# A fourth early up tile and an instruction order written by hand between the first LayerNorm and the feed-forward block, in a one-core transformer layer

## The chip, the core and the metric

The kernel runs on one core of a Trainium2 chip. Its engines are TensorE (PE in the profile, with weight loads shown as PEld), VectorE (DVE), ScalarE (ACT), GpSimd (POOL) and SyncE (SP, which here only issues DMAs). The metric is the device time of one launch in microseconds (us), taken as the median of several runs. Lower is better.

## What is computed

One diffusion-transformer layer over 1024 tokens of width 1024: two attention branches, a gated merge, a residual with LayerNorm, and a convolutional SwiGLU feed-forward block with a second LayerNorm. The change lies between the first LayerNorm and the feed-forward block:

```python
x = _layer_norm(DEEPNORM_ALPHA * x + gate1 * y, ln1_g[l], ln1_b[l])
h = x * (1.0 + scale2) + shift2
y = _conv_ffn(h, w_up[l], conv_w[l], conv_b[l], w_down[l])
x = _layer_norm(DEEPNORM_ALPHA * x + gate2 * y, ln2_g[l], ln2_b[l])

def _conv_ffn(h, w_up, conv_w, conv_b, w_down):
    u = h @ w_up                       # 1024 x 5632
    ...                                # depthwise conv of width 3 over tokens, plus conv_b
    gate, val = jnp.split(u, 2, axis=-1)
    return (jax.nn.silu(gate) * val) @ w_down
```

All data is float32. Each matrix product is done as three matmuls (`mm3`, L89): both operands are split into a rounded high part and a low remainder, and high x high, high x low and low x high are added up. So every operand needs a cast on ScalarE (L82) and a subtraction on VectorE or GpSimd (L87 for weights, L1208 for activations) before TensorE can use it.

## The kernel before

**Layout.** Features lie on the 128 partitions and tokens along the free dimension. The hidden width 2816 of the feed-forward block is cut into 22 up tiles `j`; each has a gate part (`gv` = 0) and a value part (`gv` = 1), written `u0_j` and `u1_j` here. The first three (`NCL = 3`) are plain products, each part 8 x 2 x 3 matmuls of 512 tokens (`up_mm`, L1393). The other 19 are block tiles (`up_tile`, L1498): a 2 x 2 block scheme with seven products A11, S2, S1, S3, A12, S4, A22 of 12 matmuls each (`prod`, L1486) in place of eight. Their weight operands are sums of weight blocks (`wsums`, four additions on GpSimd), cast and split by `pairs` (L1477); their activation operands are the normalized activations `B` and sums of them, `T13` and `T24`, made by `build` (L1239).

**The stage of the change.** The output projection (`y_pair`) fills `z` in three token slices, 0:512, 512:768 and 768:1024 (`LN1_S`). For each slice `ln_steps` (L1144) takes sums by tiny matmuls, broadcasts mean and scale into a PSUM tile (L1174, tile `bca` in the pool tag `sml`, two banks), and then for each of eight feature tiles applies them on VectorE and GpSimd (L1182 to L1186), makes the high part and a copy `v` on ScalarE (L1202), and the low part (L1208). Meanwhile TensorE works on `u0_0`, `u1_0` and `u0_1` for the slices that are ready (L1431 to L1436). Their sums stand in the three two-bank PSUM slots of the tag `big`. After that come `u1_1`, `u0_2` and `u1_2` over all tokens (`up_conv`, L1406), each taking a `big` slot after the convolution (`conv3`, L1363) has read the earlier part there; `gated` (L1373) multiplies gate and value and stores them. The steps of `build` hang on a clock of matmul columns (`tick`, L1130, cost `BLD = 2400`). Then all of PSUM is given back and taken anew as eight single banks for the block tiles.

**Rings.** Raw weights go through three buffers `raw`; high and low weights through two rings of four (`w` and `wd`), which the plain parts and the block tiles share. A slot is filled again only after the matmuls that read it.

**What sets the order.** TensorE's order is written by hand from L1304 on. On the other engines and on the DMA queues a planner in the framework orders the instructions: it takes them by program order as their inputs become ready in its own simulation. On the chip each engine then runs its list strictly in order. `with tc.manual_schedule(engines=...)` turns the planner off for the named engines, so that these follow the program text.

Of the kernel before, what the change touches and what calls it, by code (L numbers as in the profile page):

```python
# [13 lines left out]
P = 128  # L14
D = 1024
T = 1024
# [53 lines left out]
def layer_kernel(  # L70
# [65 lines left out]
    def hput(*names):  # L136
        for n in names:
            hfree.append(hslot.pop(n))
# [865 lines left out]
    za = tc.alloc_tile_pool(name="za", bufs=1, side="right", reuse_waits="tile")  # L1004
    wq = tc.alloc_tile_pool(name="wq", bufs=1, side="right", reuse_waits="tile")
    ps3 = tc.alloc_tile_pool(name="ps3", bufs=1, space=PSUM, reuse_waits="tile")

    hfree += [(za, f"Z{n}") for n in range(16)]

# [4 lines left out]
        return ps3.tile([P, T], F32, tag="big", name=name, bufs=3)  # L1014

    def sml(name, w=512):
        return ps3.tile([P, w], F32, tag="sml", name=name, bufs=2)

    def weight(src, nm, n=8, tag="w", he=None, le=None, rtag="raw"):
        if rtag:  # L1020
# [268 lines left out]
    def up_weights(j, gv, which=None):  # L1289
        upw[j, gv] = wring(w_up[2 * j + gv], f"wu{gv}_{j}", le=nc.vector, which=which)  # L1290
# [72 lines left out]
    def conv3(t, u, c):  # L1363
        nc.scalar.activation(t, u, AF.Identity, bias=cvb[:, c:c + 1], scale=cvw[:, c, 1:2])
        nc.vector.scalar_tensor_tensor(out=t[:, 1:T], in0=u[:, 0:T - 1], scalar=cvw[:, c, 0:1], in1=t[:, 1:T],
                                       op0=ALU.mult, op1=ALU.add)
        nc.vector.scalar_tensor_tensor(out=t[:, 0:T - 1], in0=u[:, 1:T], scalar=cvw[:, c, 2:3],
                                       in1=t[:, 0:T - 1], op0=ALU.mult, op1=ALU.add)
# [37 lines left out]
    def up_conv(j):  # L1406
        cv = []
        for gv in (0, 1):
            up_mm(j, gv, [hsl(0), hsl(1)])
            if gv == 0:  # L1410
                hslot[f"c0_{j}"] = pool, tag = cs[j % 2]
                t = pool.tile([P, T], F32, tag=tag, name=f"c0_{j}", bufs=1)
            else:
                if j == NCL - 1:
                    hput("B3_1")
                    hfree.insert(0, hfree.pop())
# [5 lines left out]
        if j:  # L1422
            later.append(f"c1_{j}")
        else:
            hput(f"c1_{j}")

    up_weights(1, 0, 1)
    up_weights(1, 1, 1)
    for j, gv in ((0, 0), (0, 1), (1, 0)):
        up_start(j, gv)  # L1430
    for si, s in enumerate(LN1_S):  # L1431
        drain((len(LN1_S) - 1 - si) * (KT + 3))
        for j, gv in ((0, 0), (0, 1), (1, 0)):
            up_mm(j, gv, [s])
            if s.stop == T:
                ups[j, gv][2].add(HALF)  # L1436
    cs = [hfree.pop(0) for _ in range(2)]
    for k in range(4):
        pend += [(BLD, fn) for fn in build(k)]
    later = []  # L1440
    for j in range(NCL):
        up_conv(j)
    drain()
    hput(*[f"B{k}_1" for k in range(3)], *later)


    ps3.release()
    ps3 = tc.alloc_tile_pool(name="ps3u", bufs=1, space=PSUM, reuse_waits="tile")

    ubanks = list(PSU)  # L1450

    def bank(name):
        n = ubanks.pop(0)
        ubanks.append(n)
        return ps3.tile([P, HALF], F32, tag=f"u{n}", name=name)

    for n in range(8):
        ps3.tile([P, HALF], F32, tag=f"u{n}", name=f"u{n}")

    def wload(j):  # L1460
        wraw[j] = [post.tile([P, 8, P], F32, tag="raw", name=f"ru{gv}_{j}", bufs=3) for gv in (0, 1)]
        for gv in (0, 1):
            nc.sync.dma_start(wraw[j][gv], w_up[2 * j + gv])
# [12 lines left out]

    def pairs(j, *names):  # L1477
        for n in names:
            if (j, n) not in wsrc:
                continue  # L1480
            pool, tag = ((wq, "w"), (post, "wd"))[npair[0] % 2]
            npair[0] += 1
            t = wtile[j, n] = pool.tile([P, 2, HALF], R32, tag=tag, name=f"w{n}_{j}", bufs=4)
            split(wsrc.pop((j, n)), t[:, 0], t[:, 1], nc.scalar, getattr(nc, UE[list(prods).index(n)]))

    def prod(j, n, o, start, stop):  # L1486
        w = wtile.pop((j, n))
        for k in range(4):
            c = slice(k * P, (k + 1) * P)
            mm3(o, (w[:, 0, c], w[:, 1, c]), opnd(prods[n], k), start and k == 0, stop and k == 3, not start)  # L1490
            tick(HALF / 0.8)

    def add(o, p, q, e=nc.vector):
        e.tensor_tensor(out=o, in0=p, in1=q, op=ALU.add)
# [1 line left out]
    lohalf, hihalf = slice(0, HALF), slice(HALF, T)  # L1496

    def up_tile(j):  # L1498
        a, b, c, d = (bank(f"{n}{j}") for n in "abcd")
# [7 lines left out]
        prod(j, "S2", b, True, True)  # L1507
        add(ve, b, pe)
        prod(j, "S1", c, True, True)
        nc.scalar.copy(uv[:, hihalf], c)  # L1510
        pairs(j, "A12", "S4", "A22")
        if j + 1 < NF:
            wload(j + 1)
            wsums(j + 1, tm)
        prod(j, "S3", d, True, True)
        add(uv[:, hihalf], d, uv[:, hihalf])
        add(uv[:, hihalf], uv[:, hihalf], ve, nc.gpsimd)
        pairs(j + 1, "A11")
        prod(j, "A12", a, False, True)
        nc.scalar.copy(ug[:, lohalf], a)  # L1520
        prod(j, "S4", c, False, True)
        add(ug[:, hihalf], c, ve)
        conv3(tg, ug, j)
        nc.scalar.activation(tg, tg, AF.Silu)
# [7 lines left out]
    wload(NCL)  # L1532
    wsums(NCL, tm)
    pairs(NCL, "A11", "S2", "S1", "S3")
    for j in range(NCL, NF):
        if j == NF - 1:
            dnext()
        up_tile(j)
# [338 lines left out]
```

## Time and profile before

| what | value |
|---|---|
| time, median of 3 runs | 1578.76 us (1578.74 to 1580.79) |
| the profiled execution, its own time | 1578.46 us |
| its span, first to last instruction | 1576.7 us |
| VectorE busy 946 to 957 us | 11.0 of 11 us |
| VectorE busy 957 to 979 us | 18.8 of 22 us |

The profile is one execution. Its page gives sums over the whole span; the views of stretches, of the chain of waits and of the order of time are cut out of the same record. Matmuls overlap in the pipeline, so the distance from one start to the next says how fast TensorE goes, not the duration of one. An idle time is put down to the engine whose semaphore came last. The stage in question runs from about 903 us (first plain product) to 979 us (first block product).

### The profile page before, as it was taken

Reading aid. Unit: us, or ns where it says so; the run is one execution under the profiler, and the core shown is the slowest. Engines: PE = TensorE matmul, PEld = TensorE weight load, DVE = VectorE, ACT = ScalarE, POOL = GpSimd, SP = SyncE. Lnnn points to the kernel's source line nnn. Section 1 sums busy time; section 2 is a strip of 40 time slices with the busy share of each in tenths; the row PEclk is TensorE's granted clock in tenths of the full one; section 3 lists DMA queues with packets and bytes.
Section 4 is the critical chain, followed back from the end, with each engine's and each line's share of the span. In section 5 each row is a group of like instructions: output and inputs, shape, how many; then the busy total and the mean of one; then the engine's idle time right before and its main releaser. Section 6 shows DMA issues by size and latency. Waiting matters only on the chain.

```text
span 1576.7 us, 22297 instructions
## 1 busy us (share of the span) xinstructions
PE 1538.4 (98%) x7804; PEld 1283.1 (81%) x7804; DVE 1199.0 (76%) x1768; ACT 813.8 (52%) x1450; POOL 740.2 (47%) x728
## 2 busy tenths in 40 slices
PE   9999999999999999989999999999999999999997
PEld 7888888888877787777688988888888888888887
DVE  6677976548888677788674788788888887657884
ACT  5323123368887667688430564444444444435552
POOL 0355423526666556555342454566667774021121
PEclk9999999999999999999999999999999999999998
DMA  9776662322247555440550222323334446996821
GB/s 372 270 234 234 224 232 90 110 79 59 63 127 158 130 134 132 115 87 18 179 174 27 92 69 96 118 96 117 109 108 118 110 113 186 367 266 210 258 101 54
DMA packets 112528, 230.00 MB, mean 146 GB/s; under 512 B 12992, under 2 KB 27840, under 8 KB 112320
## 3 DMA queue, kind: packets, MB, share of 16 engines
q1 hardware_dynamic: 97184, 199.72, 38.1%
q0 software_dynamic: 10400, 20.19, 8.4%
q10 hardware_dynamic: 4832, 8.68, 1.5%
q8 instruction: 61, 1.00, 0.3%
q14 instruction: 51, 0.42, 0.1%
HBM read 177.35 MB, written 65.86 MB: 154 GB/s over the span
## 4 chain that ended last, share of the span: by engine, by line
PE 87%; DVE 5%; ACT 3%; issue 2%; POOL 1%; DMA 0%; SPq 0%; DVEq 0%; ACTq 0%; POOLq 0%
PE ptr L611 5%; PE p L90 4%; PE p L91 4%; PE p L92 4%; PE g L90 4%; PE g L92 4%; PE g L91 4%; PE b L92 3%; PE b L91 3%; PE b L90 3%; PE av L632 2%; PE s L494 2%; PE av L633 2%; PE d L92 2%; PE c L92 2%; PE a L92 2%
## 5 line engine op out<-in xcount | busy, mean ns | idle before, releaser
L621 DVE TENSOR_TENSOR ptl<-ptr,pth 128x512 fp32r<-128x512 f32 x188 | 124.5, 684 | 28.0 <-ACT pth L620 26.0
L611 PE MATMUL ptr<-ident,p 128*128 128x128 f32 x816 | 126.8, 278 | 10.5 <-DVE ptl L621 8.2
L620 ACT CAST pth<-ptr 128x512 fp32r<-128x512 f32 x188 | 106.6, 588 | 57.8 <-PE ptr L611 34.2
L87 DVE TENSOR_TENSOR ld<-rd,hd 128x1024 fp32r<-128x1024 f32 x77 | 95.0, 1249 | 49.2 <-ACT hd L82 45.4
L506 ACT ACTIVATE p<-p,nm 128x1024 f32<-128x1024 f32 (+2 forms) x128 | 125.3, 981 | 10.7 <-DVE p L539 10.0
L611 PEld LDWEIGHTS ptr<-ident,p 128*128 128x128 f32 x816 | 93.6, 140 | 40.9 <-DVE ptl L621 13.9
L82 ACT CAST hd<-rd 128x1024 fp32r<-128x1024 f32 x77 | 79.4, 1049 | 82.2 <-PE p L92 58.4
L632 PE MATMUL av<-pth,VT 128*128 128x512 f32 x236 | 104.5, 443 | 0.7 <-ACT avs L638 0.5
L90 PE MATMUL p<-hd 128*128 128x512 f32 x264 | 103.2, 391 | 0.0
L87 POOL TENSOR_TENSOR wlg<-wg,whg 128x512 fp32r<-128x512 f32 x32 | 45.7, 1438 | 122.4 <-ACT whg L82 122.4
L92 PE MATMUL p<-hd,ld 128*128 128x512 f32 x264 | 102.7, 389 | 0.0
L91 PE MATMUL p<-ld,hd 128*128 128x512 f32 x264 | 102.7, 389 | 0.0
L90 PE MATMUL g<-hh,whg 128*128 128x512 f32 x256 | 99.9, 390 | 0.0
L92 PE MATMUL g<-hh,wlg 128*128 128x512 f32 x256 | 99.7, 389 | 0.0
L91 PE MATMUL g<-hl,whg 128*128 128x512 f32 x256 | 99.6, 389 | 0.0
L633 PE MATMUL av<-ptl,VT 128*128 128x512 f32 x236 | 97.7, 414 | 2.0 <-POOL ptl L87 1.8
L539 DVE TENSOR_SCALAR_CACHE_REDUCE p<-s,cvt,nmc 128x1024 f32<-128x1024 f32 x64 | 84.4, 1339 | 12.1 <-PE s L495 11.8
L494 PE MATMUL s<-KL,q 128*128 128x512 f32 (+2 forms) x192 | 76.0, 396 | 2.7 <-ACT p_x L506 2.0
L783 ACT ACTIVATE sg<-g,bgc 128x512 f32<-128x512 f32 x32 | 22.0, 687 | 97.0 <-PE g L92 92.0
L84 POOL TENSOR_SCALAR pth<-prw 128x512 fp32r<-128x512 f32 x48 | 31.0, 646 | 87.2 <-ACT prw L617 62.2
L495 PE MATMUL s<-KL,q 128*128 128x512 f32 (+2 forms) x192 | 71.7, 373 | 0.0
L82 ACT CAST wA<-ru 128x512 fp32r<-128x512 f32 x57 | 35.5, 623 | 67.8 <-PE d L92 36.2
(433 smaller groups left out, 5015.2 us busy)
## 6 DMA issues: line engine op xcount, KB each, us to landing
wml<-in_wmodT_dram SPq DMA_DIRECT2D x48, 512.0 KB
ru<-in_w_up_dram SPq DMA_DIRECT2D x38, 512.0 KB
rd<-td SPq DMA_DIRECT2D x55, 256.0 KB
rd<-sd SPq DMA_DIRECT2D x44, 256.0 KB
rd<-in_w_dn_dram SPq DMA_DIRECT2D x33, 256.0 KB
wm<-in_wmodT_dram SPq DMA_DIRECT2D x16, 512.0 KB
wg<-in_w_g_dram SPq DMA_DIRECT2D x32, 256.0 KB
sgd<-sg ACTq DMA_DIRECT2D x32, 256.0 KB
```

Source lines behind the costliest of these rows:

```text
L82: nc.scalar.copy(hi, src)
L87: lo_eng.tensor_tensor(out=lo, in0=src, in1=hi.bitcast(F32), op=ALU.subtract)
L90: nc.tensor.matmul(ps, a[0], b[0], start=start, stop=False, skip_group_check=resumed)
L91: nc.tensor.matmul(ps, a[0], b[1], start=False, stop=False, skip_group_check=resumed)
L92: nc.tensor.matmul(ps, a[1], b[0], start=False, stop=stop, skip_group_check=resumed)
L494: nc.tensor.matmul(o, self.q[0][:, hs], ks, start=True, stop=False)
L506: nc.scalar.activation(p, s, AF.Exp, bias=nm[:, h:h + 1], scale=scale, accum_out=sm[:, h:h + 1])
L611: nc.tensor.transpose(tr[:, h * P:(h + 1) * P], self.pslice(h, n), ident)
L620: nc.scalar.copy(hi, tr)
L621: nc.vector.tensor_tensor(out=lo, in0=tr, in1=hi.bitcast(F32), op=ALU.subtract)
L632: nc.tensor.matmul(self.av, v, hi, start=first, stop=False)
L633: nc.tensor.matmul(self.av, v, lo, start=False, stop=self.left == 0)
```

## The change

Names: `ps3s` is now a PSUM pool of its own for the two `sml` banks. Behind the last normalization step it is released, and the two banks become one tile `big4` for `u1_1`. The `BLD` clock goes, and the three engines VectorE, ScalarE and GpSimd follow the text from the builds to the end of the first block tile; in the next two block tiles ScalarE alone does.

```diff
-BLD = 2400.0
-PSU = 6, 7, 2, 3, 4, 5, 0, 1
+PSU = 4, 5, 2, 3, 0, 1, 6, 7
 ...
-    for j, gv in ((0, 0), (0, 1), (1, 0)):
+    early = (0, 0), (0, 1), (1, 0)
+    for j, gv in early:
         up_start(j, gv)
     for si, s in enumerate(LN1_S):
         drain((len(LN1_S) - 1 - si) * (KT + 3))
-        for j, gv in ((0, 0), (0, 1), (1, 0)):
+        if s.stop == T:
+            ps3s.release()
+            ps3s = tc.alloc_tile_pool(name="ps3c", bufs=1, space=PSUM, reuse_waits="tile")
+            ups[1, 1] = ps3s.tile([P, T], F32, tag="big4", name="u1_1"), upw.pop((1, 1)), set()
+            early += (1, 1),
+            up_mm(1, 1, LN1_S[:si])
+        for j, gv in early:
             up_mm(j, gv, [s])
 ...
-    for k in range(4):
-        pend += [(BLD, fn) for fn in build(k)]
-    for j in range(NCL):
-        up_conv(j)
 ...
+    with tc.manual_schedule(engines=MAN):
+        for k in (0, 1):
+            built[k][0]()
+            built[k][1]()
+        for k in (0, 1):
+            built[k][2]()
+            built[k][3]()
+        built[2][0]()
+        built[2][1]()
+        conv_in(0, 0)
+        up_weights(2, 0)
+        conv_in(0, 1)
+        up_weights(2, 1)
+        gate_out(0)
+        built[2][2]()
+        built[2][3]()
+        conv_in(1, 0)
+        built[3][0]()
+        built[3][1]()
+        wload(NCL)
+        wsums(NCL, tm)
+        built[3][2]()
+        conv_in(1, 1)
+        pairs(NCL, "A11")
+        built[3][3]()
+        pairs(NCL, "S1")
+        wfetch(NCL + 1, 0)
+        gate_out(1)
+        pairs(NCL, "S3", "S2")
+    for gv in (0, 1):
+        up_mm(2, gv, [hsl(0), hsl(1)])
 ...
     def up_tile(j):
+        first = j == NCL
+        if first:
+            ad, cb = big(f"ad{j}"), ps3s.tile([P, T], F32, tag="big4", name=f"cb{j}")
+            a, d, c, b = (t[:, h] for t in (ad, cb) for h in (lohalf, hihalf))
 ...
         prod(j, "A11", a, True, True)
         nc.scalar.copy(pe, a)
+        if first:
+            conv_in(2, 0)
+            pairs(j, "A12")
+            wload(j + 1)
+        else:
+            prod(j, "S2", b, True, True)
+            add(ve, b, pe)
         prod(j, "S1", c, True, True)
 ...
         conv3(tg, ug, j)
+        if first:
+            pairs(j + 1, "S1", "S3", "A12")
+        elif j < NCL + 3:
+            pairs(j + 1, "S2", "S1", "S3")
         nc.scalar.activation(tg, tg, AF.Silu)
         pairs(j + 1, "S2", "S1", "S3")
 ...
+    with tc.manual_schedule(engines=MAN):
+        up_tile(NCL)
+    ps3s.release()
+    ps3.release()
 ...
+    with tc.manual_schedule(engines={mybir.EngineType.Activation}):
+        for j in (NCL + 1, NCL + 2):
+            up_tile(j)
+    for j in range(NCL + 3, NF):
```

`conv_in` and `gate_out` are the two halves of the former `up_conv`. In the first block tile the seven products come in the order A11, S1, S3, S2, A12, S4, A22, and the convolutions of `u0_2` and `u1_2` are placed between them. The number of matmuls stays the same, but the second half of `u1_1` is now done in two slices of 256 tokens.

More of the change, by code (lines that the diff above doesn't have):

```diff
@@ L1432, in layer_kernel, with wfetch @@
         drain((len(LN1_S) - 1 - si) * (KT + 3))
-        for j, gv in ((0, 0), (0, 1), (1, 0)):
+        if s.stop == T:
[5 more added lines that the diff above has]
+        for j, gv in early:
             up_mm(j, gv, [s])
             if s.stop == T:
-                ups[j, gv][2].add(HALF)
-    cs = [hfree.pop(0) for _ in range(2)]
-    for k in range(4):
-        pend += [(BLD, fn) for fn in build(k)]
-    later = []
-    for j in range(NCL):
-        up_conv(j)
[L1443 to L1458, printed above, removed]
+                ups[j, gv][2].update((0, HALF))
+    def wfetch(j, gv):
+        r = post.tile([P, 8, P], F32, tag="raw", name=f"ru{gv}_{j}", bufs=3)
+        nc.sync.dma_start(r, w_up[2 * j + gv])
+        wraw.setdefault(j, []).append(r)
     def wload(j):
-        wraw[j] = [post.tile([P, 8, P], F32, tag="raw", name=f"ru{gv}_{j}", bufs=3) for gv in (0, 1)]
-        for gv in (0, 1):
-            nc.sync.dma_start(wraw[j][gv], w_up[2 * j + gv])
+        for gv in range(len(wraw.get(j, ())), 2):
+            wfetch(j, gv)
         (a11, a12), (_, a22) = [[r[:, 4 * n:4 * n + 4].rearrange("p a b -> p (a b)") for n in (0, 1)]
@@ L1484, in pairs, with conv_in, gate_out, bank @@
             split(wsrc.pop((j, n)), t[:, 0], t[:, 1], nc.scalar, getattr(nc, UE[list(prods).index(n)]))
+    cs = [hfree.pop(0) for _ in range(2)]
+    built = [build(k) for k in range(4)]
+    cv = {}
+    def conv_in(j, gv):
+        if gv == 0:
+            hslot[f"c0_{j}"] = pool, tag = cs[j % 2]
+            t = pool.tile([P, T], F32, tag=tag, name=f"c0_{j}", bufs=1)
+        else:
+            t = ht(f"c1_{j}")
+        conv3(t, ups.pop((j, gv))[0] if (j, gv) in ups else u2[gv], gv * NF + j)
+        cv[j, gv] = t
+    def gate_out(j):
+        g, v = cv.pop((j, 0)), cv.pop((j, 1))
+        nc.scalar.activation(g, g, AF.Silu)
+        gated(j, g, v)
+        hput(f"c1_{j}")
+    MAN = {mybir.EngineType.DVE, mybir.EngineType.Activation, mybir.EngineType.Pool}
+    with tc.manual_schedule(engines=MAN):
[29 more added lines that the diff above has]
+        up_mm(2, gv, [hsl(0), hsl(1)])
+    u2 = [ups.pop((2, gv))[0] for gv in (0, 1)]
+    drain()
+    hput(*[f"B{k}_1" for k in range(4)])
+    hfree[:] = hfree[-4:] + hfree[:-4]
+    ubanks = list(PSU)
+    def bank(name):
+        n = ubanks.pop(0)
+        ubanks.append(n)
+        return ps3.tile([P, HALF], F32, tag=f"u{n}", name=name)
     def prod(j, n, o, start, stop):
@@ L1506, in up_tile @@
         nc.scalar.copy(pe, a)
[L1507 to L1508 removed]
+        if first:
+            conv_in(2, 0)
+            pairs(j, "A12")
+            wload(j + 1)
+        else:
+            prod(j, "S2", b, True, True)
+            add(ve, b, pe)
         prod(j, "S1", c, True, True)
         nc.scalar.copy(uv[:, hihalf], c)
[L1511 to L1516 removed]
+        if first:
+            prod(j, "S3", d, True, True)
+            add(uv[:, hihalf], d, uv[:, hihalf])
+            pairs(j, "S4")
+            conv_in(2, 1)
+            prod(j, "S2", b, True, True)
+            add(ve, b, pe)
+            pairs(j, "A22")
+            gate_out(2)
+            wsums(j + 1, tm)
+        else:
+            pairs(j, "A12", "S4", "A22")
+            if j + 1 < NF:
+                wload(j + 1)
+                wsums(j + 1, tm)
+            prod(j, "S3", d, True, True)
+            add(uv[:, hihalf], d, uv[:, hihalf])
         add(uv[:, hihalf], uv[:, hihalf], ve, nc.gpsimd)
[L1518 removed]
+        if not first:
+            pairs(j + 1, "A11")
         prod(j, "A12", a, False, True)
         nc.scalar.copy(ug[:, lohalf], a)
+        if first:
+            pairs(j + 1, "A11")
         prod(j, "S4", c, False, True)
         add(ug[:, hihalf], c, ve)
+        if first:
+            pairs(j + 1, "S2")
         conv3(tg, ug, j)
+        if first:
+            pairs(j + 1, "S1", "S3", "A12")
+        elif j < NCL + 3:
+            pairs(j + 1, "S2", "S1", "S3")
         nc.scalar.activation(tg, tg, AF.Silu)
@@ L1530, in up_tile @@
         hput(*[f"{n}{j}" for n in ("pv", "ug", "uv", "tv")])
[L1532 to L1535, printed above, removed]
+    with tc.manual_schedule(engines=MAN):
+        up_tile(NCL)
+    ps3s.release()
+    ps3.release()
+    ps3 = tc.alloc_tile_pool(name="ps3u", bufs=1, space=PSUM, reuse_waits="tile")
+    for n in range(8):
+        ps3.tile([P, HALF], F32, tag=f"u{n}", name=f"u{n}")
+    with tc.manual_schedule(engines={mybir.EngineType.Activation}):
+        for j in (NCL + 1, NCL + 2):
+            up_tile(j)
+    for j in range(NCL + 3, NF):
         if j == NF - 1:
```

14 lines of the change are left out of this document (5 added, 9 removed).

## The prediction

> **What bounds the kernel now.** I read the page first: the busy time of the engines and the chain that ended last.
>
> ```profile
> span 1576.7 us, 22297 instructions
> PE 1538.4 (98%) x7804; PEld 1283.1 (81%) x7804; DVE 1199.0 (76%) x1768; ACT 813.8 (52%) x1450; POOL 740.2 (47%) x728
> PE 87%; DVE 5%; ACT 3%; issue 2%; POOL 1%; DMA 0%; SPq 0%; DVEq 0%; ACTq 0%; POOLq 0%
> ```
>
> TensorE is busy 98% of the span and makes up 87% of the chain. The number of matmuls doesn't change, so time can only come from where TensorE waits or runs slowly. Next, the view of waits, for TensorE from 900 us to the end. It has one row (waited for; us in total, times, longest):
>
> ```profile
> PE u L91 <- DVE B L1208: 2.9, 1, 2.9
> ```
>
> One plain product waited for the low half of a normalized activation. Behind it the view of stretches shows no gap (length, busy time of PE, PEld, DVE, ACT, POOL, then the granted TensorE clock, DMA share, GB/s):
>
> ```profile
> 980.00:1340.00 360.00, 360.00 (x1590) 298.20 (x1589) 305.68 (x270) 172.21 (x243) 235.22 (x136) 1.00 0.41 118
> 1340.00:1560.00 220.00, 220.00 (x1124) 187.88 (x1122) 152.55 (x181) 105.95 (x130) 35.72 (x30) 1.00 0.69 216
> ```
>
> So TensorE is full from 980 to 1560 us, and whatever is won or lost before 980 arrives at the end unchanged, as long as the later stage keeps its order and lead. The place itself, in TensorE's order of time (start, duration) and in stretches:
>
> ```profile
> 923.02 0.28 PE L90 MATMUL u<-B,hwu 128*128 128x256 f32 x1
> ...
> 932.73 0.28 PE L90 MATMUL u<-B,hwu 128*128 128x256 f32 x1
> 935.90 0.58 PE L91 MATMUL u<-B,hwu 128*128 128x256 f32 x1 [2.88 <-DVE B L1208]
> ...
> 946.00 0.28 PE L92 MATMUL u<-B,lwu 128*128 128x256 f32 x1
> 946.12 0.40 PE L90 MATMUL u<-B,hwu 128*128 128x512 f32 x1
> ...
> 957.03 0.39 PE L90 MATMUL u<-B,hwu 128*128 128x512 f32 x1
> ...
> 978.79 0.39 PE L90 MATMUL a<-B,wA 128*128 128x512 f32 x1
> ...
> 997.83 0.39 PE L90 MATMUL a<-B,wA 128*128 128x512 f32 x1
> ```
>
> ```profile
> 932.00:936.00 4.00, 1.12 (x10) 0.91 (x8) 4.00 (x5) 3.22 (x5) 4.00 (x4) 0.90 0.10 33
> 936.00:942.00 6.00, 6.00 (x28) 6.00 (x29) 6.00 (x5) 4.46 (x5) 3.35 (x3) 0.50 0.00 0
> 942.00:946.00 4.00, 4.00 (x35) 4.00 (x34) 4.00 (x5) 2.92 (x4) 1.52 (x1) 1.00 0.00 0
> ```
>
> The wait has a tail: for the 6 us after it the granted clock is 0.50, and only 28 matmuls start where the next 4 us hold 35. It is a wait and a slow start in one.
>
> **The loss, as a number.** From 923.02 to 946.12 stand 144 matmuls of 256 columns (three parts, two slices, 24 each): 23.10 us. The 82 that start from 923.02 to 932.73 run at full clock, 9.71 / 81 = 0.120 us apart. At that pace 144 take 17.27 us. The loss is 23.10 - 17.27 = **5.83 us**: about 3.05 idle (932.73 to 935.90, less one step of 0.12) and 2.8 in slow clock.
>
> **What the change does there.** It puts 24 matmuls of 512 and 24 of 256 columns of `u1_1` between the slices. From 946.12 to 957.03 the 48 wide matmuls of `u1_1` took 10.91 us, 0.227 each; so the inserted work is 24 x 0.227 + 24 x 0.12 = 8.3 us against a wait of 2.9. It begins at 923.02 + 72 x 0.12 = 931.7 and ends at 940.0. What it needs is late next, so I look at VectorE's order of time before:
>
> ```profile
> 929.23 0.74 DVE L1182 TENSOR_TENSOR z<-z,bca 128x256 f32<-128x256 f32 x2
> 929.89 1.11 DVE L1208 TENSOR_TENSOR t<-v,t 128x512 f32<-128x512 f32 x1
> ...
> 933.22 1.75 DVE L1208 TENSOR_TENSOR t<-v,t 128x512 f32<-128x512 f32 x1
> 934.89 2.37 DVE L1208 TENSOR_TENSOR B<-v,B 128x256 fp32r<-128x256 f32 x2
> ...
> 942.28 1.27 DVE L1365 SCALAR_TENSOR_TENSOR c<-u,cvt,c 128x1023 f32<-128x1023 f32 x1
> ...
> 946.46 1.21 DVE L87 TENSOR_TENSOR lwu<-rwu,hwu 128x1024 fp32r<-128x1024 f32 x1
> ...
> 966.35 2.31 DVE L1208 TENSOR_TENSOR T24l<-t,T24h 128x1024 fp32r<-128x1024 f32 x1
> ...
> 969.79 2.98 DVE L87 TENSOR_TENSOR wS<-s,wS 128x512 fp32r<-128x512 f32 x3
> ```
>
> Two things. The banks of `big4` are those of `bca`, last read at 929.23 + 0.74 = 930.0, so `u1_1` finds them free 1.7 us ahead. And the last low halves, done at 937.3 even with the build steps ahead of them (929.89 to 933.22), are wanted only from 940.0. The wait goes, and with it the slow clock.
>
> The price: 24 matmuls of 512 columns become 48 of 256: 48 x 0.12 - 24 x 0.227 = 5.76 - 5.44 = **+0.3 us**.
>
> Net: 5.83 - 0.32 = **5.5 us** earlier. The new timetable for TensorE: last slices 940.0 to 951.5, `u0_2` to 962.4, `u1_2` to 973.3, where the first block product started at 978.79 before. Everything behind it must hold a date 5.5 us earlier, from these costs (lines by form, 920 to 980 us: count | busy, mean ns), a weight load from SP's issue to its first reader, and the steady state (1000 to 1320 us):
>
> ```profile
> L1365 DVE SCALAR_TENSOR_TENSOR c<-u,cvt,c 128x1023 f32<-128x1023 f32 x5 | 6.4, 1272 | 0.0
> L1208 DVE TENSOR_TENSOR T24l<-t,T24h 128x1024 fp32r<-128x1024 f32 x4 | 5.9, 1487 | 0.0
> L1208 DVE TENSOR_TENSOR t<-v,t 128x512 f32<-128x512 f32 x4 | 5.3, 1321 | 0.0
> ```
> ```profile
> 973.44 0.33 SPq L1463 DMA_DIRECT2D ru<-in_w_up_dram  x1
> ```
> ```profile
> 977.23 1.29 POOL L1208 TENSOR_TENSOR s<-ru 128x512 f32<-128x512 f32 x1 [5.61 <-DMA ru<-in_w_up_dram]
> ```
> ```profile
> L87 DVE TENSOR_TENSOR wS<-s,wS 128x512 fp32r<-128x512 f32 x51 | 48.7, 980 | 0.0
> L82 ACT CAST wS<-s 128x512 fp32r<-128x512 f32 x67 | 40.1, 621 | 35.9 <-POOL s L1208 35.5 <-PE b L92 0.4
> L1365 DVE SCALAR_TENSOR_TENSOR tv<-uv,cvt,tv 128x1023 f32<-128x1023 f32 x17 | 39.2, 2307 | 0.0
> L1364 ACT ACTIVATE tg<-ug,cvt 128x1024 f32<-128x1024 f32 x17 | 21.2, 1245 | 2.9 <-DVE ug L1494 2.9
> L1365 DVE SCALAR_TENSOR_TENSOR tg<-ug,cvt,tg 128x1023 f32<-128x1023 f32 x16 | 22.1, 1380 | 22.1 <-ACT tg L1364 19.4 <-DMA ru<-in_w_up_dram 2.7
> ```
>
> *`u0_2` at 951.5.* It needs the slot of `u0_0`, free when its convolution is read out, and the low weights of (2,0). Before, VectorE reached that convolution at 942.28. Now two more `t` steps and one `T24l` stand ahead: 2 x 1.32 + 1.49 = 4.1 us with the means. Then 946.4 + 2 x 1.27 = 948.9, and the low weights (1.21; their ring slot is free when `u0_1` ends, 940.0 + 3 x 24 x 0.12 = 948.6) at 950.2. **Margin 1.3 us.** `u1_2` needs its slot at 962.4: one convolution more, near 953; covered.
>
> *First block tile at 973.3.* Written order queues all VectorE work: builds, four convolutions, two gatings, four weight lows. The same set was done at 969.79 + 2.98 = 972.8 before. It is wanted by S1 at 973.3 + 2.7 = 976.0, S3 at 978.7 and S2 at 981.5 (2.72 us a product, a seventh of 997.83 - 978.79 = 19.04). S1's operand comes before the second gating in the text. Covered by 3 us or more, with two in-order waits inside: GpSimd's four sums now stand behind its subtraction of the fourth build, which waits for VectorE, and ScalarE's casts S3 and S2 stand behind the second silu. On SP's queue the next tile's loads wait for freed `raw` buffers; a load lands in 977.23 - 973.44 = 3.8 us, and the second half of tile 4's weights, freed near 981, is there by 985, for a product (S2) at 995.
>
> *Tiles 4 and 5, ScalarE as written.* The cast of S2 for the next tile stands behind the convolution's start, which waits for S4. From S4's end: add 0.7, activation 1.25, then VectorE's two convolution steps (2 x 1.38, with the cast of 0.62 beside them) and the low half, 0.98: 5.7 us. TensorE has A22 and A11 in hand, 5.44 us, and asks for the low half two matmuls (0.45) later: 5.9. **Margin 0.2 us**, the thinnest. If all is contended (2.31 a step) it is 0.7 + 1.25 + 4.62 + 0.98 = 7.55, late by 1.7 per tile, twice. If the planner puts the low half ahead of the second step, the margin is 1.6. Below nothing these waits can't go: no other TensorE wait is left to remove. I take zero, nearest to the means, and keep 3.4 us for the range.
>
> The sum, against the profiled execution: 1578.46 - 5.5 = 1572.95. The median of the runs lies 0.30 above it, at 1578.76: **1573.3 us**.
>
> [...]
>
> **The rivals.**
> - *VectorE is the new bound at `u0_2` or in the first block tile.* For it: it is busy 4.00 of 4 and 6.00 of 6 us at the seam, and the margin of 1.3 rests on means. Against: the same work fitted before. With the `t` and `T24l` steps at 1.75, 1.75 and 2.31 it is late by 0.4; each further microsecond costs one. Two to three late: 1575.3 to 1576.3.
> - *Casts too late in tiles 4 and 5, without a clock drop.* Two waits of up to 1.7: up to 1576.7.
> - *The same place, with the clock lost: slower.* If each of the two waits passes the 2.9 us that the trace shows to be enough, each costs 2.9 + 2.8: 1573.3 + 11.4 = 1584.7. One alone gives 1579.0. It decides from about 1.2 us beyond the contended end. For it: strict order in three places at once. Against: TensorE has 5.44 us of products in hand there.
> - *The change doesn't fill the gap.* If `u1_1` has to wait for the last normalization steps, through the reused banks, the wait stays: 1578.8, unchanged. Against: 1.7 us of margin.
>
> **How the numbers follow.** Forecast, 5.5 us gained with at most 1.5 given back (1572.0 to 1574.9): 0.64. VectorE late: 0.11. Casts late: 0.10. Gap not filled or one clock drop: 0.08. Two drops: 0.07. The measurement can tell about 0.2%, 3.2 us, from no change; so faster means below 1575.6. That is the forecast and half of the two milder rivals, 0.74. Same: the other halves and most of the fourth, 0.17. Slower: the two drops and the rest, 0.09. The range goes from 1571.6 (the forecast with the spread of runs) to 1578.0, which leaves the last two rivals out.
>
> **What would show it.** Right: the row "u L91 <- B L1208" is gone; no 0.50 clock between 930 and 950; `u1_1` starts near 932 and the first block product near 973; no TensorE wait behind it. Wrong: a TensorE wait put down to `lwu` or to a convolution's read near 951, to `wS` or `wA` from 975 to 1035, or a stretch at 0.50 there.

## The result, and the profile after

| | median of the runs, us | lowest to highest |
|---|---|---|
| before | 1578.75 | 1577.06 to 1580.79 |
| after | 1588.66 | 1586.36 to 1591.68 |

The ratio is 1.0061, with a 95% interval of 1.005 to 1.0072: the change makes the kernel **9.9 us slower**, where 5.5 us faster was forecast. The profiled execution took 1591.68 us. Its page, span and busy times:

```profile
span 1589.9 us, 22346 instructions
PE 1541.7 (97%) x7828; PEld 1283.5 (81%) x7828; DVE 1198.0 (75%) x1768; ACT 810.9 (51%) x1450; POOL 735.9 (46%) x728
```

The busy times are those of before within 5 us on every engine; the span is 13.2 us longer. So no engine has more work; TensorE waits more. The view of waits of after, TensorE from 850 us to the end (engine, waiting instruction <- releaser: us in total, times, longest; two rows of 0.4 and 0.2 are left out), where before had the one row of `u L91` behind 900 us:

```profile
PE c L91 <- POOL wS L86: 4.2, 1, 4.2
PE b L89 <- ACT wS L81: 2.2, 1, 2.2
PE c L89 <- ACT uv L1566: 1.9, 1, 1.9
PE d L89 <- DVE uv L1540: 1.7, 2, 1.1
PE b L91 <- DVE wS L86: 0.5, 1, 0.5
```

The wait at the seam is gone, as forecast. In its place stand waits of block products `a` to `d`: for split weights (`wS`), and for banks whose sum ScalarE or VectorE has not yet moved out (`uv`). The view of stretches tells where (columns as in the prediction; the number behind PE's busy time is the count of matmuls that started). After, then before:

```profile
920.00:980.00 60.00, 60.00 (x357) 53.61 (x356) 50.90 (x56) 30.22 (x41) 25.05 (x19) 1.00 0.21 71
980.00:1000.00 20.00, 20.00 (x90) 16.57 (x89) 19.54 (x17) 9.79 (x15) 12.31 (x7) 1.00 0.31 106
1000.00:1020.00 20.00, 15.79 (x60) 12.53 (x59) 10.69 (x11) 6.14 (x10) 11.21 (x7) 0.83 0.32 105
...
1040.00:1060.00 20.00, 15.36 (x60) 11.66 (x59) 12.61 (x12) 8.57 (x15) 14.46 (x10) 0.91 0.17 53
1060.00:1100.00 40.00, 38.26 (x168) 31.00 (x167) 37.20 (x33) 18.78 (x28) 25.59 (x14) 1.00 0.32 105
```

```profile
920.00:980.00 60.00, 57.12 (x309) 50.56 (x308) 52.29 (x55) 33.26 (x44) 29.20 (x22) 0.94 0.23 79
...
1000.00:1020.00 20.00, 20.00 (x90) 16.57 (x89) 15.75 (x16) 9.15 (x14) 11.55 (x8) 1.00 0.32 106
```

From 920 to 980 TensorE of after has neither an idle time nor a low clock. But in two stretches of 20 us behind 1000 it starts 60 matmuls where a full stretch holds 90, and the granted clock falls to 0.83 and 0.91 there. Both effects can be cut apart by the starts of four matmuls: the first plain matmul of 256 columns, the first block product, the same product one tile on, and the same five tiles on (tile 8). After:

```profile
925.12 0.28 PE L89 MATMUL u<-B,hwu 128*128 128x256 f32 x1
...
975.41 0.39 PE L89 MATMUL ad<-B,wA 128*128 128x512 f32 x1
...
994.45 0.39 PE L89 MATMUL a<-B,wA 128*128 128x512 f32 x1
...
1086.60 0.39 PE L89 MATMUL a<-B,wA 128*128 128x512 f32 x1
```

**The seam** took 975.41 - 925.12 = 50.29 us, against 978.79 - 923.02 = 55.77 before: 5.48 us gained. **The first block tile** took 994.45 - 975.41 = 19.04, as in the steady state: nothing lost. **Five block tiles** took 1086.60 - 975.41 = 111.19 against 5 x 19.04 = 95.20 before: **15.99 us lost**, all of it in tiles 4, 6 and 7. The recorded waits of the view above come to 10.5 us of that; the rest, 5.5 us, goes in matmuls that start further apart behind the waits (0.43 us behind the first, where the full pace is 0.227). Together that is 10.5 us slower, close to the 9.9 of the medians. (The profiled execution came to the seam 2.1 us later than the one of before, 925.12 against 923.02. That is ahead of the part that was reordered, and the profiles of the experiments come there between 921.71 and 924.03. 10.5 + 2.1 leaves 0.6 of the 13.2.)

The first of the long waits, followed back through the order of time of all engines (start, duration, engine; in brackets the idle time ahead of an instruction and what ended it; TensorE's rows stand last):

```profile
996.27 2.19 DVE L1367 SCALAR_TENSOR_TENSOR tg<-ug,cvt,tg 128x1023 f32<-128x1023 f32 x1
...
999.60 0.68 DVE L86 TENSOR_TENSOR wA<-ru,wA 128x512 fp32r<-128x512 f32 x1
...
1000.34 0.33 SPq L1440 DMA_DIRECT2D ru<-in_w_up_dram  x1
...
1003.99 2.01 POOL L1208 TENSOR_TENSOR s<-ru 128x512 f32<-128x512 f32 x1 [6.60 <-DMA ru<-in_w_up_dram]
...
1010.00 1.59 POOL L1208 TENSOR_TENSOR s<-ru,s 128x512 f32<-128x512 f32 x1
1011.55 1.26 POOL L86 TENSOR_TENSOR wS<-s,wS 128x512 fp32r<-128x512 f32 x1
...
1008.27 0.39 PE L90 MATMUL c<-B,wS 128*128 128x512 f32 x1
1012.87 0.79 PE L91 MATMUL c<-B,wS 128*128 128x512 f32 x1 [4.21 <-POOL wS L86]
1013.46 0.63 PE L89 MATMUL c<-B,wS 128*128 128x512 f32 x1
```

Read it from the end. Product S4 of tile 4 wants its low half at 1008.5. GpSimd makes it (1011.55), but only after the four weight sums of tile **5**, which stand ahead of it in its list and began at 1003.99, when a raw weight had landed. That load was issued at 1000.34. It could not go earlier: the ring `raw` has three buffers, and the buffer that it takes is free when VectorE has made the low half of tile 4's A12, at 999.60 + 0.68 = 1000.28. And that low half stood on VectorE behind the two convolution steps of the block tile before it and two other low halves. So a *load of the next tile* that comes late stops a product of *this* tile. The tail is then the slow clock: from 1013.46 on the matmuls start 0.43 us apart, where 0.227 is the full pace, and the granted clock from 1013 to 1018 is 0.52.

### The profile page after: what moved, and what is told of

It reads as the page before. It is cut to its first block, busy times and chain, and to the rows that moved or that the text cites. A ratio compares the mean times of both kernels' runs of the same rounds, so it can differ in the third digit from the quotient of the medians.

```text
span 1589.9 us, 22346 instructions
## 1 busy us (share of the span) xinstructions
PE 1541.7 (97%) x7828; PEld 1283.5 (81%) x7828; DVE 1198.0 (75%) x1768; ACT 810.9 (51%) x1450; POOL 735.9 (46%) x728
## 5 line engine op out<-in xcount | busy, mean ns | idle before, releaser
L91 PE MATMUL p<-hd,ld 128*128 128x512 f32 x264 | 102.8, 389 | 0.0
L91 PE MATMUL g<-hh,wlg 128*128 128x512 f32 x256 | 99.7, 389 | 0.0
L81 ACT CAST wS<-s 128x512 fp32r<-128x512 f32 x76 | 45.2, 620 | 54.7 <-POOL s L1208 53.9
```

Source lines behind the costliest of these rows:

```text
L81: nc.scalar.copy(hi, src)
L91: nc.tensor.matmul(ps, a[1], b[0], start=False, stop=stop, skip_group_check=resumed)
```

## The experiments

Two theories stood against each other; each expectation below was written before its run, and those of the later runs know the earlier ones. **The lead:** the seam's gain is real, and the written order of the block tiles makes their operand chain (load, sums, cast, low half) start later, so that TensorE catches up with it; then either one of the written parts does it, or each of them. **A shortage:** the order is not at fault; an earlier start of the block tiles, or the fourth early tile, simply asks for more than VectorE, GpSimd or the loads give, and giving the order back to the planner helps little.

For each run the table has the seam and the five block tiles, cut as above from its profile, its median, and the interval of its ratio to the runs of before on the same chip. The runs were spread over chips on which before took 1577.98 to 1579.17 us, so a difference of medians between two rows can be off by about 1 us.

| run | seam, us | loss in five block tiles, us | median, us | ratio to before, 95% interval |
|---|---|---|---|---|
| before | 55.77 | 0 | 1578.75 | |
| after | 50.29 | 15.99 | 1588.66 | 1.005 to 1.0072 |
| e1_act_planned | 50.29 | 7.52 | 1582.57 | 1.0012 to 1.0031 |
| e2_pool_written | 50.29 | 14.23 | 1586.39 | 1.0029 to 1.0063 |
| e3_fourth_alone | 60.02 | 0.41 | 1583.00 | 1.0013 to 1.0035 |
| e4_a12_early | 50.29 | 10.16 | 1583.30 | 1.002 to 1.0039 |
| e5_tiles_planned | 50.29 | 1.59 | 1575.10 | 0.9971 to 0.999 |
| e7_45_written | 50.29 | 11.98 | 1585.35 | 1.0027 to 1.0055 |
| e8_no_fourth | 53.43 | 0 | 1576.89 | 0.9976 to 0.9994 |
| e9_tile3_act | 50.28 | 1.25 | 1574.43 | 0.9964 to 0.9985 |

### ScalarE back to the planner in tiles 4 and 5

```diff
-    with tc.manual_schedule(engines={mybir.EngineType.Activation}):
+    if True:
         for j in (NCL + 1, NCL + 2):
             up_tile(j)
```

> The changed kernel with ScalarE left to the planner in block tiles 4 and 5 (the rest of the change stays). Theory G (GpSimd's list in tile 4 holds the four weight sums of tile 5 ahead of the low half of S4, and the sums wait for a load; ScalarE's cast of S4 was done 4 us before TensorE asked): the planner may cast S4 earlier, so its low half may come ahead of the sums; 1573 to 1583 us, and if a TensorE wait of 3 us or more stays in tile 4 it is again put down to GpSimd. Theory S (ScalarE's written order in tiles 4 and 5 is what starves TensorE): 1574 or less, with no TensorE wait over 0.5 us behind 950 us. Theory V (the written first block tile has used up the lead of the weight operands, whoever orders tiles 4 and 5): 1584 or more.

It took 1582.57 us, 6.1 less than after, but still slower than before. The time lies in G's range, but the wait is put down to ScalarE and not to GpSimd; S (1574 or less) and V (1584 or more) are both missed. More than half of the loss goes, and one wait is left, in tile 4. ScalarE's order of time and TensorE's in this run:

```profile
1009.46 1.14 ACT L81 CAST wS<-s 128x512 fp32r<-128x512 f32 x2 [6.44 <-POOL s L1208]
1010.50 0.58 ACT L1566 COPY uv<-c 128x512 f32<-128x512 f32 x1
...
1011.13 0.80 PE L89 MATMUL c<-B,wS 128*128 128x512 f32 x1 [4.77 <-ACT uv L1566]
```

The place is new; the origin is again a late load. The planner put the casts of tile 5 ahead of the copy that empties bank `c`. The casts wait 6.44 us for the sums of tile 5, which stand behind a load issued at 999.49. That is just behind A22's low half on GpSimd (997.72 + 1.74 = 999.46); A12's on VectorE ended at 1000.61, so the load seems to have taken the other buffer here. Both low halves are late, though tiles 4 and 5 are planned, and that points at the written order of the first block tile. The run that leaves it out follows below.

### GpSimd in written order too

```diff
-    with tc.manual_schedule(engines={mybir.EngineType.Activation}):
+    with tc.manual_schedule(engines={mybir.EngineType.Activation, mybir.EngineType.Pool}):
```

> The changed kernel with GpSimd too in written order in block tiles 4 and 5, so that the low halves of S4 and A22 stand ahead of the next tile's four sums. Theory G: the 4.2 us wait at S4 of tile 4 and the slow clock behind it go (6.9 us in all); the low half of S4 is done near 1005, TensorE asks at 1008. The later waits (4.7 us in tile 6, 2.9 in tile 7, 1.2 in tile 8) may stay or go: 1573 to 1582 us. Theory S: ScalarE's order is unchanged, so the time stays at 1586 to 1589. Theory V: the wait moves to another product of tiles 4 to 6 and the time stays at 1584 or more.

It took 1586.39 us, within 2.3 of after, where theory G had at most 1582. This puts S4's low half of tile 4 ahead of the next tile's sums. The wait of 4.2 for it is gone, and others take its place further on:

```profile
PE c L89 <- ACT uv L1566: 3.8, 1, 3.8
PE a L91 <- DVE wA L86: 2.8, 1, 2.8
PE c L91 <- DVE wS L86: 0.9, 1, 0.9
```

Tile 4 loses 0.59 now in place of 6.80, and tiles 5 and 6 lose 13.64. Taking one instruction out of the way of one operand does not give the lead back to the others.

### The fourth early tile on the kernel before, all else planned

```diff
 ...
-        for j, gv in ((0, 0), (0, 1), (1, 0)):
+        early = ((0, 0), (0, 1), (1, 0))
+        if s.stop == T:
+            ps3s.release()
+            ps3s = tc.alloc_tile_pool(name="ps3c", bufs=1, space=PSUM, reuse_waits="tile")
+            ups[1, 1] = ps3s.tile([P, T], F32, tag="big4", name="u1_1"), upw.pop((1, 1)), set()
+            early += (1, 1),
+            up_mm(1, 1, LN1_S[:si])
+        for j, gv in early:
 ...
```

> The kernel before with the fourth early up tile alone: the two small PSUM banks become one tile for u1_1, which runs ahead of the last slice. Builds on the clock, planner's order and eight single banks as before. If the wait of 2.9 us and the slow clock behind it are worth 5.8 us and the split of 24 wide matmuls costs 0.3: 1573.2 us (1572 to 1574.5), with no TensorE wait behind 900 us. Rival: the gain isn't there, or the builds, now with fewer plain products ahead of the first block tile, come too late: 1577 or more, with a TensorE wait near 950 to 975.

It took 1583.00 us, slower than before: the fill alone does not pay. The wait of 2.9 between the slices is gone, but the view of waits has two new rows at the seam, which grows to 60.02 us:

```profile
PE u L90 <- DVE c L1368: 4.8, 1, 4.8
PE u L92 <- DVE lwu L87: 1.0, 1, 1.0
```

`u0_2` now asks 5 us earlier for the bank of `u0_0`. The planner has put all steps of the builds but one ahead of that convolution on VectorE, which has the bank read out only at 956.2. The rival of the prediction that VectorE would be late at `u0_2` is what happens here, without the written seam. In the block tiles this run loses 0.41 us: the fourth early tile by itself takes little from them.

### The cast and low half of A12 of tile 4 ahead of the convolution

```diff
         if first:
-            pairs(j + 1, "S2")
+            pairs(j + 1, "S2", "A12")
         conv3(tg, ug, j)
         if first:
-            pairs(j + 1, "S1", "S3", "A12")
+            pairs(j + 1, "S1", "S3")
```

> The changed kernel; in the first block tile the cast and low half of the next tile's A12 stand ahead of the convolution instead of behind it, so that VectorE frees the raw buffer near 994 instead of 1000, and the second half of tile 5's weights lands near 998 instead of 1004. Theory L (the chain low half of A12, load, four sums on GpSimd, low half of S4 is what TensorE waited for in tile 4): the sums end near 1006, the wait of 4.2 us at S4 goes or falls under 1 us, its slow clock goes, and the time is 1578 to 1583 us (the waits of tiles 6 to 8, 8.8 us with theirs, may shrink too). Rival: the load isn't what sets the date, and the wait stays above 3 us: 1586 to 1589.

It took 1583.30 us, 5.4 less than after. The load that was issued at 1000.34 is issued at 992.43 here, and the wait of 4.2 in tile 4's S4 is gone: the chain that was read backwards above is confirmed for that wait. The rest of the expectation was missed, the range by 0.3 us. The rows that are left are of tiles 4, 6 and 7:

```profile
PE c L89 <- ACT uv L1566: 3.0, 1, 3.0
PE d L89 <- DVE uv L1540: 2.4, 2, 2.1
```

One of them, 2.1 us, is in tile 4 itself, of bank `d`, and it too has a slow clock behind it (0.76 from 1009 to 1016), so that tile 4 still loses 3.98 of 6.80. This one order buys 5.8 of the 15.99 us and no more.

### Written order at the seam alone

The written part ends with the second gating. The last two convolutions and all block tiles go back to the planner, with the product order and the function `up_tile` of before. The eight single banks go round in an order of their own (`PSU = 0, 1, 6, 7, 2, 3, 4, 5`), in this run and the three that follow.

```diff
         pairs(NCL, "S3", "S2")
 ...
+    conv_in(2, 0)
+    conv_in(2, 1)
+    gate_out(2)
+    ps3s.release()
+    ps3.release()
 ...
-    with tc.manual_schedule(engines=MAN):
-        up_tile(NCL)
 ...
-    with tc.manual_schedule(engines={mybir.EngineType.Activation}):
-        for j in (NCL + 1, NCL + 2):
-            up_tile(j)
-    for j in range(NCL + 3, NF):
+    for j in range(NCL, NF):
 ...
         up_tile(j)
```

> The fourth early up tile and the written order from the builds to the second gating stay; all block tiles, and the third plain convolution and gating ahead of them, go back to the planner, to the product order of before and to eight single banks. Theory V (the written first block tile starts the operand chain of the next tiles later, and with it goes the lead of about a tile that the planner had built up): the lead is back, TensorE has no wait over 0.5 us behind 950 us, 1572.5 to 1575 us. Rival (the planner misjudges the busy seam, as it did at u0_2 in the run of the fourth tile alone): a TensorE wait of 2 to 5 us in tile 3 or 4, 1577 us or more.

It took 1575.10 us, faster than before (0.998, interval 0.9971 to 0.999) and 13.6 less than after. The seam is the same 50.29, and the block tiles lose 1.59, nearly all of it by one wait in the first of them. That wait, and 0.1 us of the time, lie outside what theory V expected; the rival's wait of 2 to 5 us didn't come.

```profile
PE c L89 <- ACT uv L1565: 1.1, 1, 1.1
```

This run speaks against the shortage: the block tiles start as early as in after, with the same fourth tile, loads and sums, and TensorE runs through them. The low half of tile 4's A12 and the load behind it, in the order of time of this run:

```profile
989.95 0.68 DVE L86 TENSOR_TENSOR wA<-ru,wA 128x512 fp32r<-128x512 f32 x1
...
990.70 16.00 SPq L1440 DMA_DIRECT2D ru<-in_w_up_dram  x2
...
994.23 2.00 POOL L1208 TENSOR_TENSOR s<-ru 128x512 f32<-128x512 f32 x1 [1.25 <-DMA ru<-in_w_up_dram]
```

### ScalarE written in tiles 4 and 5 only

The run before, with the change's rule for these two tiles, the casts ahead of the silu included.

```diff
         conv3(tg, ug, j)
+        if NCL < j < NCL + 3:
+            pairs(j + 1, "S2", "S1", "S3")
         nc.scalar.activation(tg, tg, AF.Silu)
 ...
-    for j in range(NCL, NF):
+    up_tile(NCL)
+    with tc.manual_schedule(engines={mybir.EngineType.Activation}):
+        for j in (NCL + 1, NCL + 2):
+            up_tile(j)
+    for j in range(NCL + 3, NF):
 ...
         up_tile(j)
```

> The kernel with all block tiles planned (1575.1 us), but with ScalarE in written order in tiles 4 and 5 as the change has it, the casts ahead of the silu there too. It tells the written tiles 4 and 5 from the written first block tile. Theory V1 (the first block tile alone costs the lead; tiles 4 and 5 only inherit it): 1574 to 1577 us. Theory V2 (the text casts S4 and A22 of a tile only behind the copy of c in that same tile, so that the lead shrinks to about 5 us whatever the tile before did): TensorE waits of 2 to 5 us in tiles 4 to 6, and 1579 to 1588 us.

It took 1585.35 us: 10.3 more than without it (9.4, if each is taken against its own runs of before), as theory V2 had it. ScalarE, VectorE and SP in this run, at the same low half and load:

```profile
1003.22 0.59 ACT L1565 COPY uv<-c 128x512 f32<-128x512 f32 x1 [4.12 <-PE c L91]
1003.71 0.62 ACT L81 CAST wA<-ru 128x512 fp32r<-128x512 f32 x1
...
1004.36 0.69 DVE L86 TENSOR_TENSOR wA<-ru,wA 128x512 fp32r<-128x512 f32 x1 [1.58 <-ACT wA L81]
...
1005.42 2.91 SPq L1440 DMA_DIRECT2D ru<-in_w_up_dram  x2
```

Here the order by itself is seen. In the text the casts of A12, S4 and A22 stand behind the copy of bank `c`. In written order ScalarE idles 4.12 us in front of that copy until TensorE has filled the bank, with three casts behind it whose data lie ready. The planner had made the first of them at 988.48. So the buffer comes free at 1005.05 in place of 990.63, and the load goes 14.1 us later, counted in each run from its first block product.

With e1, e5 and after, this makes a square of the two written parts. (The lower row has the banks of the change, the upper one those of e5.) Loss in the five block tiles, us:

| | tiles 4 and 5 planned | tiles 4 and 5 written on ScalarE |
|---|---|---|
| first block tile planned | 1.59 | 11.98 |
| first block tile written | 7.52 | 15.99 |

Each part loses by itself (5.9 and 10.4 over the first field), and together they lose 14.4, not much less than the sum. The first part contains the other order of the seven products and the other banks as well, which were not tried apart from the written order; the second contains the place of the casts as well as the order.

### Written order on ScalarE in the first block tile, casts early; and that without the fourth tile

e9 keeps e5, removes its wait of 1.1 by putting the copy of bank `c` ahead of the casts of the next tile, and has the casts of the first tile all issued before the tile.

```diff
             wsums(j + 1, tm)
+            if j == NCL:
+                pairs(j + 1, "A11", "S2", "S1", "S3")
 ...
-    for j in range(NCL, NF):
+    pairs(NCL, "A12", "S4", "A22")
+    with tc.manual_schedule(engines={mybir.EngineType.Activation}):
+        up_tile(NCL)
+    for j in range(NCL + 1, NF):
```

> The kernel with all block tiles planned, except that ScalarE follows the text in the first block tile, with the copy of c ahead of the next tile's casts and those casts ahead of the rest. The 1.1 us for which S4 waited for that copy goes, the lead stays: 1573.5 to 1574.5 us, 0.2 to 0.3% under the kernel before. Rival (another engine is as late as that copy was): a wait of about 1 us at the same place, 1575 us.

It took 1574.43 us, the fastest here (0.9975 of before, 0.9964 to 0.9985). The wait of 1.1 is gone; rows of 0.5 and 0.2 are left, and the block tiles lose 1.25. From e5 it can't be told apart by time. So written order as such need not lose, at least on ScalarE in this one tile: here the casts are written *ahead of* what they must not wait for.

e8 is e9 without the fourth early tile, so the two differ by the fill alone:

```diff
-            early += (1, 1),
-            up_mm(1, 1, LN1_S[:si])
 ...
+    up_mm(1, 1, [hsl(0), hsl(1)])
```

> The same kernel with all block tiles planned, without the fourth early tile: u1_1 runs behind the slices, all of it in matmuls of 512, in the banks that the change gives it. If the wait of 2.9 us and the half clock behind it are what the early tile removes: the row comes back with 2.5 to 3.2 us, the granted clock is 0.50 for some 6 us, and the time is 1575.1 + 5.5 = 1580.6 us (1579 to 1582). Rival (the wait was due to build steps ahead of the last low halves, which the written order has moved): no wait and no half clock, 1574 to 1576.

It took 1576.89 us, between the two expectations. Its seam is 53.43 us, so the fill is worth 3.15 of the 5.5 us there, and **the written order of the seam by itself gains 2.34**. The whole 5.5 had been put down to the fill, and that part of the reading falls. Of the 3.15 not all is kept: e8 loses nothing in the block tiles, where e9 loses 1.25, and the medians of the two, from one chip, are 2.5 us apart. The same slice waits, but for less long:

```profile
PE u L90 <- DVE B L1208: 1.7, 1, 1.7
```

The kernel before had 2.9 there. On VectorE three `t` steps stand ahead of the first of the two last low halves in e8, where the planner had put four (the rows at 929.89 to 933.22 in the prediction, the fourth of 1.75 us).

## Why the prediction was wrong, and where it was right

- **The loss at the seam (5.83), the price (0.3), net 5.5: right in size.** 5.48 was measured, 50.29 us in six kernels. One source was missed: the written order gives 2.34 of it without the fill (e8), and the fill adds the other 3.15 at its price of 0.3. The fill also takes the wait away without the written order (e3), but there a longer wait at `u0_2` takes its place. That the sum came out is no luck: the 5.83 was all that could be removed at this place, and both together remove it.
- **`u0_2` with a margin of 1.3: right.** VectorE ended the convolution of `u0_0` at 950.7 and the low weights at 952.1. Both lie 1.8 and 1.9 us behind the forecast 948.9 and 950.2, and the seam itself began 2.1 later. No wait stands there. Where the planner orders this stretch, e3 shows the same margin broken by 4.8 us.
- **First block tile, covered by 3 us or more: right as far as it went.** The tile took 19.04 us. The part looked at whether its *own* operands come in time, and stopped there. What its order does to the *next* tile's load wasn't asked: with tiles 4 and 5 planned it costs 5.9 us (e1 against e5).
- **"Tiles 4 and 5, ScalarE as written. Margin 0.2 ... I take zero, and keep 3.4 us for the range": this is the step that failed.** It followed one chain, the cast of S2 for the next tile behind the convolution. The first long wait was for another operand: S4's low half on GpSimd, behind the sums of the next tile, behind a load, behind a buffer that A12's low half frees. The rows for this were at hand: three `raw` buffers, the four sums, and the load of 3.8 us. What was missing is the question by how much each operand was *ahead* before. For the S2 cast of tile 4 it was 18.4 us (cast 982.19, product 1000.55); in after it is 5.4 (991.79, 997.17). For S2 of tile 5 it was 17.2 and is 3.5. In e5 the two are 10.0 and 15.9. The term that the forecast put at zero, with 3.4 us kept for the range, measured 15.99. The S2 chain that it had priced did hold in tile 5; S2 of tile 6 waited 2.25 us, for sums behind a late load and not for the convolution. A margin of a few tenths for one operand, in a stage whose lead was nearly a tile of 19.04, was itself the sign that the order had spent the lead.
- **"As long as the later stage keeps its order and lead"** was the condition under which a gain ahead of 980 arrives. It was written down and not worked out. It broke in after. Where it nearly held, much of the 5.5 us reached the end: against the runs of before on the same chip e5 is 2.9 us faster (1577.98 to 1575.10) and e9 4.4 (1578.79 to 1574.43).
- **The rivals.** *VectorE the new bound*: not in after, but true of the fill without the written seam (e3). *Casts late without a clock drop*: the waits came, but the clock fell with them (0.83 and 0.91 in the two stretches of 20 us). *The same place, with the clock lost*, 1584.7, slower: this is the one nearest to what happened. Its sign was right and its place in part: it had the S2 chain in tiles 4 and 5, and there were six waits, in tiles 4, 6 and 7, two of them over 2 us. The sign of being wrong that was named, a wait for `wS` from 975 to 1035, is the one at 1012.87. *The gap isn't filled*: false.
- **The contended convolution steps (1576.7).** They were not it. The four steps for `tg` in tiles 4 and 5 of after, behind S4, took 1.27 or 1.28 us each: the two of tile 4 (1019.59, 1021.39) beside no GpSimd instruction, the two of tile 5 (1038.87, 1045.58) with one beside their ends (from 1039.32 and 1046.57) for 0.83 and 0.28 us. In before, from 1000 to 1320 us, the steps of `tv` took 1.28 us in the two places where no GpSimd instruction overlapped them (1004.88, 1024.96), and 2.20 to 2.32 everywhere else, where one did. `tv` has its inputs in SBUF in all of them, so the 2.31 of the prediction is no cost of SBUF inputs alone.

One date by which the kernels can be compared is that load, for tile 5. Its issue, counted from the first block product, us:

| kernel | low half of A12 made | load issued | behind the first block product | lost in tiles 3, 4, 5, 6, 7 |
|---|---|---|---|---|
| before | 991.2 | 991.25 | 12.5 | 0, 0, 0, 0, 0 |
| e3 | 995.8 | 995.82 | 12.9 | 0.4, 0, 0, 0, 0 |
| e8 | 993.3 | 993.33 | 16.4 | 0, 0, 0, 0, 0 |
| e5 | 990.6 | 990.70 | 17.0 | 1.5, 0.1, 0, 0, 0 |
| e9 | 990.8 | 990.97 | 19.0 | 0.4, 0.9, 0, 0, 0 |
| e4 | 992.4 | 992.43 | 20.4 | 0, 4.0, 0.1, 5.5, 0.6 |
| after | 1000.3 | 1000.34 | 24.9 | 0, 6.8, 0, 7.8, 1.4 |
| e2 | 997.7 | 997.74 | 24.9 | 0, 0.6, 4.7, 9.0, 0 |
| e1 | 1000.6 | 999.49 | 26.0 | 0, 7.5, 0, 0, 0 |
| e7 | 1005.1 | 1005.42 | 31.1 | 1.5, 0, 1.3, 7.8, 1.3 |

In the kernels with up to 19 us the stage still runs nearly at its pace; in those beyond 20 it doesn't. How much is lost, and where, is not a matter of this load alone: in e2 and e7 tile 4 loses almost nothing with it, and the loss comes in tiles 5 to 7. In e1, with the planner, one wait of 4.8 with its slow clock (0.83 from 1000 to 1020) is all, and every tile from 5 on takes 19.04 again. In after and e7 it comes back: there the load of tile 6 is late in its turn. The order of time of after shows it, behind stores on the same queue:

```profile
1032.54 0.37 SPq L1380 DMA_DIRECT2D td<-tv  x1
1033.00 1.31 SPq L1440 DMA_DIRECT2D ru<-in_w_up_dram  x2
...
1039.32 1.98 POOL L1208 TENSOR_TENSOR s<-ru 128x512 f32<-128x512 f32 x1 [3.99 <-DMA ru<-in_w_up_dram]
...
1043.79 1.66 ACT L81 CAST wS<-s 128x512 fp32r<-128x512 f32 x3 [4.96 <-POOL s L1208]
...
1044.46 0.50 PE L89 MATMUL b<-T24h,wS 128*128 128x512 f32 x1 [2.25 <-ACT wS L81]
```

The last store of the finished tile is issued at 1032.54, when VectorE has made its data (1030.70 + 1.78), and two loads directly behind it from 1033.00. A12's low half of tile 5 had been done at 1030.78, so as it looks the first load lost 2.2 us behind that store. The sums begin 6.3 us after its issue, where 3.7 passed for the load above (1000.34 to 1003.99). From 1034 to 1037 the DMA engines are busy 0.95 of the time or more; whether the stores in front make the load slower, or the second load beside it, was not tried. A ring of four raw buffers, which might remove the tie between A12's low half and the load, was not tried either.

## What to carry to other kernels

Before an order is written by hand, measure in the trace how far each operand is ahead of its use, and follow each ring buffer that the order touches to the load that waits for it. A lead that the planner built up (18.4 us for the S2 cast of tile 4 in before) looks like idle time, and the text in program order spent it here (5.4 in after): in e7 three casts with ready data stood behind a copy that waited 4.12 us for TensorE. Where a stretch gains by the hand (here the seam, where e3 loses 4.3 us without it and e5 gains 5.5 with it), end the written part with it, and put everything whose data is ready ahead of the first instruction that waits.

## What the runs showed of the hardware

The slow clock also followed a wait shorter than the 2.88 us of before, and it didn't always begin at once. In e8 a wait of 1.74 us has a stretch behind it with a granted clock of 0.66:

```profile
935.00:940.00 5.00, 4.74 (x27) 4.74 (x28) 5.00 (x6) 4.35 (x6) 3.21 (x3) 0.66 0.00 0
```

In e4, TensorE's order of time, a wait of 2.12 us is followed by 1.3 us at nearly the full pace and only then by the slow one, which lasts to 1014.1:

```profile
1009.81 0.47 PE L89 MATMUL d<-T24h,wA 128*128 128x512 f32 x1 [2.12 <-DVE uv L1540]
1010.12 0.40 PE L90 MATMUL d<-T24l,wA 128*128 128x512 f32 x1
...
1011.15 0.63 PE L91 MATMUL d<-T24h,wA 128*128 128x512 f32 x1
1011.58 0.63 PE L89 MATMUL d<-T24h,wA 128*128 128x512 f32 x1
```

Against these stand a wait of 1.56 us in before (order of time, then the stretch behind it), with the clock at 1.00, and one of 1.88 us in tile 6 of after:

```profile
707.91 0.63 PE L611 MATMUL ptr<-ident,p 128*128 128x128 f32 x4 [1.56 <-DVE ptl L621]
```

```profile
708.00:714.00 6.00, 6.00 (x34) 4.63 (x35) 4.82 (x9) 5.71 (x14) 1.41 (x3) 1.00 0.02 5
```

```profile
1059.63 0.50 PE L89 MATMUL c<-B,wS 128*128 128x512 f32 x1 [1.88 <-ACT uv L1566]
```

Behind the latter the matmuls start 0.23 us apart from 1059.97 on, and the stretch from 1060 to 1100 shown with the result has a granted clock of 1.00.

In the profiles of these ten kernels, from 850 us on, ten waits were above 2 us (2.12 to 4.80), and each had the tail behind it. Of those below, the one of 1.74 had it; the one of 1.88, one of 1.63 in e7 (at 1054.59) and the shorter ones outside a tail did not. So between 1.7 and 1.9 us the length alone did not decide here. The tail took 3 to 6 us of half pace; in e3, where a second wait of 1.04 us falls into it, 8. What else decides was not shown.
